# Reciprocal softmax sums applied to the outputs of two attention mixers, and a compression layer with the activations as the stationary operand

## Chip, cores and metric

The kernel runs on one core of one Trainium2 chip. The metric is the device time of one execution in microseconds; the time before is the median of three runs, 2323.13 us (2322.97 to 2323.58).

## What is computed

One sequence of 512 positions and 1024 features, in fp32, goes through two layers of a first block (compressed, selected and windowed attention, a linear recurrence and a convolution) and then through a second block of two layers, each with a mixer, a cross attention and a feed-forward part. The change touches two pieces of this. The compression, in each layer of the first block, for keys and for values:

```
def compress(kv, pos, w1, w2):
    blk = (kv[:, :, idx] + pos).reshape(B, N_KV, n_cmp, L_CMP * HEAD_DIM)
    return jax.nn.silu(blk @ w1) @ w2
...
kc = compress(k_c, cmp_pos[0], cmp_w1[0], cmp_w2[0])
vc = compress(v_c, cmp_pos[1], cmp_w1[1], cmp_w2[1])
```

There are 31 windows of 32 positions for each of two heads, so `blk @ w1` has an inner size of 2048 and 256 outputs. And the attention of the two mixers (two branches of 8 heads each):

```
s = jnp.einsum('bqhgd,bkhd->bhgqk', q_blk, k, preferred_element_type=jnp.float32) * scale
p = jax.nn.softmax(s, axis=-1).astype(v.dtype)
return jnp.einsum('bhgqk,bkhd->bqhgd', p, v)
```

The first mixer has a dense branch and a windowed branch with a sink; the second has a dense branch with a rotary part and a neighbourhood branch with a bias.

## The kernel before, in words

Activations lie with features on partitions and positions along the free dimension. `Net.build` (L1571) runs the stages in turn: `b0` and `b1` (two layers of the first block), `ab` (first mixer), `x0` (cross attention), `f0` (feed-forward), `cd` (second mixer), `x1`, `f1`. Python code issues instructions in program order, and a scheduling layer then puts each engine's instructions into a fixed order; on the chip each engine works through its own list and waits by semaphores.

A dense product (`dense_tile`) takes 8 blocks of 128x128 weights and for each three matmuls, high by high, high by low and low by high part (L410 to L412). `weights` (L414) loads a chunk of 8 blocks, and ScalarE and VectorE (or POOL) split it into `wh` (L432) and `wl` (L365). With `raw=True` the chunk is used in fp32 as it is; an fp32 matmul stands as two records in the trace.

`compress` (L1033) projects keys and values, adds the position terms and lays the windows out as `t2`, 128 partitions by 2 heads by 512. For each of keys and values it then does the first layer: for each half `h` of the 256 outputs and each of 16 offsets `a` one matmul with a 128x128 weight block as the stationary and 64 windows (stride 16) as the moving operand (L1063), into 64 columns of one PSUM bank. ScalarE's tanh follows. The generator yields every 8 matmuls, and strings of letters (`FIRST`, `SECOND`) say in which order the parts of the block take turns. The convolution's 31 taps run on VectorE at low priority.

`attn` (L721) handles two heads at a time, in two steps of two blocks of 128 query rows. A step issues the score matmuls (L743) into the three `s` banks, VectorE takes the row minimum of the negated scores (L754, or L750 with a mask), ScalarE the exponential with its row sum `sm` (L377), and VectorE the reciprocal `sc` (L763). The second half of a step, `attn_back` (L779), is held back by one step: it multiplies `p` by `sc` (L372, called at L793), transposes `p` in 128x128 blocks into one of two `t` banks (L798), copies that to `ptt` (L805, ScalarE), and multiplies by the values into the only `o` bank (L813), 64 partitions a head. After both steps `out_to` (L828) splits the bank into `yh` (ScalarE, L395) and `yl` (VectorE, L365), which feed the output projection.

The number `cp` in the table `CFG` says how many of 8 copies from `t` VectorE makes instead of ScalarE. `memory` (L1445) is issued after a mixer's last branch: eight casts `mh` on ScalarE (L377) and eight `ml` on VectorE (L368) for the cross attention. Then the rest of the output projection (`residual`) runs.

Of the kernel before, what the change touches and what calls it, by code (L numbers as in the profile page):

```python
# [61 lines left out]
def plan():  # L62
# [9 lines left out]
    for l in range(DEPTH):  # L72
        w = ("w_in", (l,))
        dense(f"glu{l}", *w, [c for _, _, c in _cols_in1()[:8]], kt(8))
        dense(f"ul{l}", *w, [_r(UL0 + P * c, P) for c in range(4)], kt(8))
        dense(f"kcvc{l}", *w, [_r(KC0, P), _r(VC0, P)], kt(8))
        dense(f"zl{l}", *w, [_r(ZL0 + P * c, P) for c in range(4)], kt(8))
        dense(f"zc{l}", *w, [_r(ZC0 + P * c, P) for c in range(4)], kt(8))
        dense(f"qk{l}", *w, [_r(KS0, P), _r(KW0, P)] + [_pair(Q0, j) for j in range(4)], kt(8))
        ph[f"vg{l}"] = [_blk(*w, kr, c) for kr in kt(8) for c in (_r(VS0, P), _r(VW0, P), pad24)]  # L80
        dense(f"zn{l}", *w, [_pair(ZN0, j) for j in range(4)], kt(8))
        for kv in range(2):
            ph[f"c1{l}{kv}"] = [
                _blk("cmp_w1", (l, kv),
                     np.concatenate([_r(64 * a, 64), _r(64 * (a + 16), 64)]), _r(P * h, P))
                for h in range(2) for a in range(16)]
        ph[f"c2{l}"] = (
            [_blk("cmp_w2", (l, 0), kr, np.concatenate([_r(0, 64), _r(0, 64)])) for kr in kt(2)]
            + [_blk("cmp_w2", (l, 1), kr, np.concatenate([_r(0, 64), -np.ones(64, np.int64)]))
               for kr in kt(2)])  # L90
        ph[f"lru{l}"] = [("bd", key, l, c) for c in range(4) for key in ("lru_w_a", "lru_w_i")]
        dense(f"pw2{l}", "conv_w_pw2", (l,), [_r(P * n, P) for n in range(4)], kt(4))
        nsa_rows = [_pair(0, j) for j in range(4)]
        for nm, rows in (("oc", [_r(1024 + P * k, P) for k in range(4)]),
                         ("ol", [_r(512 + P * k, P) for k in range(4)]),
                         ("ona", nsa_rows[:2]), ("onb", nsa_rows[2:])):
            dense(f"{nm}{l}", "w_out", (l,), [_r(P * n, P) for n in range(8)], rows)
# [135 lines left out]
def build_consts():  # L233
    c = Cols()
    i = np.arange(P)
    c.add("ident", np.eye(P))
    c.add("ones", np.ones((P, 1)))
# [49 lines left out]
class Net:  # L287
# [14 lines left out]
        "a": dict(lay="msssstto", spare="msss", dense="ms", tok="ssss", stat="t", ahead=1, pv=-200, sc="vvvv", cp=0, low=-4000, wp=0),  # L302
        "x": dict(lay="mmssttoo", spare="mmss", dense="ms", tok="mmss", stat="t", ahead=1, pv=-200, sc="avav", cp=0, low=-4000, wp=0),
        "f": dict(lay="mmssttoo", spare="mmss", dense="ms", tok="mmoo", stat="o", ahead=1, pv=-200, sc="avav", cp=0, low=-4000, wp=0),
        "c": dict(lay="msssstto", spare="msss", dense="ms", tok="ssss", stat="t", ahead=1, pv=-200, sc="vvvv", cp=0, low=-4000, wp=0),
# [108 lines left out]
    def weights(self, name, raw=False, keep=0):  # L414
# [5 lines left out]
        for c in range(-(-nb // cs)):  # L420
# [15 lines left out]
            for b in range(n // P):  # L436
                yield wr[:, b * P:(b + 1) * P] if raw else (wh, wl, b * P)
# [283 lines left out]
    def attn(self, heads, jr, start, stop, M, done=None, mask=None, gate=None, sink=None, order=(0, 2), pre=None):  # L721
# [7 lines left out]
        for pr in order:  # L729
# [36 lines left out]
            ends = (start and pr == order[0], stop and pr == order[1])  # L766
            step = [pre] if pre and pr == order[0] else []
# [11 lines left out]
    def attn_back(self, heads, ii, pt, sc, jr, start, stop):  # L779
        nc, pr = self.nc, ii[0]  # L780
        pts = []
        for n in range(len(heads)):
            ptt = self.pt("ptt", [P, NQ, 2 * P], F32)
            pts.append(ptt)
            for a, i in enumerate(ii):
                j0, j1 = jr(i)
                nj = j1 - j0 + 1
                p, c = pt[n, a], sc[:, n, a:a + 1]
                e = self.c["sc"][2 * n + a]
                if e == "a":  # L790
# [37 lines left out]
    def out_to(self, ys, box):  # L828
        def done():
            y = (self.r("z", "yh"), self.r("z", "yl"))  # L830
            self.split(y[0], y[1], box[0])
            ys.append(y)

        return done
# [198 lines left out]
    def compress(self, l, xhl):  # L1033
# [24 lines left out]
        for kv in range(2):  # L1058
            w = self.weights(f"c1{l}{kv}", raw=True)
            ps = self.ps("t")[:, :128]  # L1060
            for h in range(2):
                for a in range(16):
                    nc.tensor.matmul(ps[:, 64 * h:64 * h + 64], next(w), t2s[kv][:, :, a],  # L1063
                                     start=a == 0, stop=a == 15)
                    if a % 8 == 7 and h + a < 16:
                        yield
# [145 lines left out]
    def mixer_ab(self):  # L1212
# [56 lines left out]
        def band_mask(i):  # L1269
            return band[:, P if i == 0 else 0:256 if i == 3 else 384]  # L1270

        def branch(br, q, k, filler):
            ys = []
            for j in range(4):
                box, take, row = self.outs()
                hs = []
# [7 lines left out]
                if br == 0:  # L1284
                    steps = self.attn(hs, lambda i: (0, 3), True, True, 64, self.out_to(ys, box), pre=take)
                else:
                    sink = par("sink", 0, 8)[:, j::4].unsqueeze(2).to_broadcast([P, 2, 2])
                    steps = self.attn(hs, lambda i: (max(0, i - 1), min(3, i + 1)), True, True, 64, self.out_to(ys, box),
                                      pre=take, mask=lambda n, i: band_mask(i), sink=sink)
# [27 lines left out]
    def mixer_cd(self):  # L1317
# [28 lines left out]
        def d_attn(p, qkv):  # L1346
            q, k, v = qkv
            box, take, row = self.outs()
            hs, sts = [], []
# [8 lines left out]
            yield from self.attn(hs, full, True, True, 64, self.out_to(ys, box), pre=take,  # L1358
# [43 lines left out]
        def c_attn(p, fq, fk, v):  # L1402
            box, take, row = self.outs()
            hs = []
# [3 lines left out]
            yield from self.attn(hs, full, True, True, 64, self.out_to(yc, box), pre=take)  # L1408
# [224 lines left out]
```

## Time and profile before

| | |
|---|---|
| median of three runs | 2323.13 us |
| the profiled execution | 2331.09 us |
| its span, first to last instruction | 2329.3 us |
| TensorE matmul busy | 2186.1 us (94%) |
| VectorE busy | 1463.1 us (63%) |
| ScalarE busy | 961.4 us (41%) |
| POOL busy | 452.0 us (19%) |
| instructions | 29296 |

Busy time is the time in which at least one instruction of the engine runs. Matmul records overlap, since the array takes the next one before the last has left it, so the step from one start to the next says what a matmul costs. PE stands for TensorE's matmuls, PEld for its weight loads, DVE for VectorE, ACT for ScalarE, POOL for GpSimd. The letter L and a number is a line of the kernel; helpers such as `self.add` or `self.act` record their own line.

### The profile page before, as it was taken

Reading aid. Unit: us, or ns where it says so; the run is one execution under the profiler, and the core shown is the slowest. Engines: PE = TensorE matmul, PEld = TensorE weight load, DVE = VectorE, ACT = ScalarE, POOL = GpSimd, SP = SyncE. Lnnn points to the kernel's source line nnn. Section 1 sums busy time; section 2 is a strip of 40 time slices with the busy share of each in tenths; the row PEclk is TensorE's granted clock in tenths of the full one; section 3 lists DMA queues with packets and bytes.
Section 4 is the critical chain, followed back from the end, with each engine's and each line's share of the span. In section 5 each row is a group of like instructions: output and inputs, shape, how many; then the busy total and the mean of one; then the engine's idle time right before and its main releaser. Section 6 shows DMA issues by size and latency. Waiting matters only on the chain. (4 is left out here: it accounts for less than half of the span.)

```text
span 2329.3 us, 29296 instructions
## 1 busy us (share of the span) xinstructions
PE 2186.1 (94%) x11052; PEld 1739.5 (75%) x11052; DVE 1463.1 (63%) x2496; ACT 961.4 (41%) x1823; POOL 452.0 (19%) x452
## 2 busy tenths in 40 slices
PE   8898899999988999998999999999998899999998
PEld 6677766777776668666878888877766688888887
DVE  8997676598876664786565544454665555554454
ACT  4422365434234653475453222233566444322223
POOL 4533421343333133111020000011100102000002
PEclk9999899999989999999999999999999999999999
DMA  4243210233331012311323333332312132333332
GB/s 142 92 136 89 62 54 28 73 104 102 107 95 48 27 58 71 97 46 46 118 81 100 91 99 92 98 91 82 93 48 74 46 109 73 100 95 96 97 94 91
DMA packets 61436, 194.73 MB, mean 84 GB/s; under 512 B 8432, under 2 KB 10480, under 8 KB 61296
## 3 DMA queue, kind: packets, MB, share of 16 engines
q1 hardware_dynamic: 52848, 179.75, 25.7%
q10 hardware_dynamic: 8448, 13.12, 2.1%
q8 instruction: 87, 1.43, 0.3%
q14 instruction: 53, 0.43, 0.1%
HBM read 182.61 MB, written 2.10 MB: 79 GB/s over the span
## 5 line engine op out<-in xcount | busy, mean ns | idle before, releaser
L432 ACT CAST wh<-wr 128x1024 fp32r<-128x1024 f32 (+2 forms) x312 | 322.7, 1034 | 688.2 <-DMA wr<-ws 595.9
L365 DVE TENSOR_TENSOR wl<-wr,wh 128x1024 fp32r<-128x1024 f32 (+1 forms) x232 | 290.2, 1251 | 316.0 <-PE ps_m L411 143.2
L410 PE MATMUL ps_m<-xh,wh 128*128 128x512 f32 x792 | 322.8, 408 | 28.6 <-DVE z L368 12.1
L412 PE MATMUL ps_m<-xh,wl 128*128 128x512 f32 x792 | 319.2, 403 | 3.1 <-POOL wl L365 2.0
L411 PE MATMUL ps_m<-xl,wh 128*128 128x512 f32 x792 | 317.8, 401 | 2.2 <-DVE xl L368 2.2
L412 PE MATMUL ps_s<-xh,wl 128*128 128x512 f32 x696 | 274.7, 395 | 7.8 <-DVE wl L365 6.9
L365 POOL TENSOR_TENSOR wl<-wr,wh 128x1024 fp32r<-128x1024 f32 (+2 forms) x80 | 192.7, 2409 | 429.8 <-PE ps_m L411 229.5
L410 PE MATMUL ps_s<-xh,wh 128*128 128x512 f32 x696 | 274.9, 395 | 0.0
L411 PE MATMUL ps_s<-xl,wh 128*128 128x512 f32 x696 | 272.8, 392 | 0.0
L362 POOL TENSOR_TENSOR sq<-sq 128x512 f32<-128x512 f32 (+1 forms) x62 | 87.2, 1407 | 949.2 <-ACT sq L377 949.2
L410 PEld LDWEIGHTS ps_m<-xh,wh 128*128 128x128 f32 x792 | 154.2, 195 | 67.2 <-DVE z L368 13.3
L377 ACT ACTIVATE p<-ps_s,mn 128x512 f32<-128x512 f32 (+3 forms) x288 | 166.0, 580 | 58.4 <-PE ps_t L798 31.1
L412 PEld LDWEIGHTS ps_m<-xh,wl 128*128 128x128 f32 x792 | 153.7, 194 | 38.8 <-DVE wl L365 3.3
L411 PEld LDWEIGHTS ps_m<-xl,wh 128*128 128x128 f32 x792 | 153.6, 194 | 36.3 <-DVE xl L368 4.0
L368 DVE SCALAR_TENSOR_TENSOR ps_s<-up,params,ps_s 128x512 f32<-128x512 f32 x232 | 170.6, 750 | 2.7
L805 ACT COPY ptt<-ps_t 128x512 f32<-128x512 f32 (+3 forms) x288 | 131.7, 476 | 82.3 <-PE ps_t L798 80.5
L412 PEld LDWEIGHTS ps_s<-xh,wl 128*128 128x128 f32 x696 | 131.6, 189 | 38.2 <-DVE wl L365 9.4
L411 PEld LDWEIGHTS ps_s<-xl,wh 128*128 128x128 f32 x696 | 132.0, 190 | 28.2 <-issue 0.4
L410 PEld LDWEIGHTS ps_s<-xh,wh 128*128 128x128 f32 x696 | 132.1, 190 | 27.5 <-issue 0.4
L798 PE MATMUL ps_t<-consts,p 128*128 128x128 f32 x848 | 135.8, 282 | 3.7 <-ACT ptt L805 3.0
L798 PEld LDWEIGHTS ps_t<-consts,p 128*128 128x128 f32 x848 | 98.1, 141 | 44.7 <-ACT ptt L805 12.8
L362 DVE TENSOR_TENSOR X<-ps_m,X 128x512 f32<-128x512 f32 (+1 forms) x114 | 76.1, 668 | 75.1 <-PE ps_m L412 74.9
(511 smaller groups left out, 4168.9 us busy)
## 6 DMA issues: line engine op xcount, KB each, us to landing
wr<-ws SPq DMA_DIRECT2D x318, 512.0 KB, 3.6
strip<-strips ACTq DMA_DIRECT2D x8, 480.0 KB, 4.4
wr<-ws SPq DMA_DIRECT2D x8, 384.0 KB, 3.6
X<-x SPq DMA_DIRECT2D x8, 256.0 KB, 4.9
mem<-mem SPq DMA_DIRECT2D x8, 256.0 KB, 2.9
wr<-ws SPq DMA_DIRECT2D x7, 256.0 KB, 3.1
tab<-tables SPq DMA_DIRECT2D x6, 256.0 KB, 3.1
out_dram<-ox SPq DMA_DIRECT2D x8, 128.0 KB, 1.7
```

Source lines behind the costliest of these rows:

```text
L362: (eng or self.nc.vector).tensor_tensor(out=out, in0=a, in1=b, op=ALU.add)
L365: (eng or self.nc.vector).tensor_tensor(out=out, in0=a, in1=b, op=ALU.subtract)
L368: self.nc.vector.scalar_tensor_tensor(out=out, in0=a, scalar=s, in1=b, op0=op0, op1=op1)
L377: return self.nc.scalar.activation(out, in_, func, **k)
L410: mm(out, ah, bh, start=first, stop=False)
L411: mm(out, ah, bl, start=False, stop=False)
L412: return mm(out, al, bh, start=False, stop=last)
L432: nc.scalar.copy(wh[:, :n], wr[:, :n])
L798: nc.tensor.transpose(t[:, j * P:(j + 1) * P], p[:, j * P:(j + 1) * P], self.con("ident"))
L805: nc.scalar.copy(dst, src)
```

## The change

**Compression.** The weights' order in memory changes so that both column halves of an offset lie side by side. The windows of one offset (64 columns, stride 16) become the stationary operand and the 256 weight columns the moving one. Even offsets go to PSUM partitions 0 to 63, odd ones to 64 to 127. ScalarE copies the two partial sums, and two matmuls with a constant `fold` (two identities of 64 on top of each other) add them and turn them back.

**Mixers.** In the two mixers `p` is not multiplied any more. `attn` keeps the reciprocals of both steps in `inv`, and `out_to` broadcasts them with eight matmuls against the identity into a `t` bank (64 partitions a head, 128 columns a block), copies that to SBUF on ScalarE, multiplies the `o` bank by it on VectorE and splits the product. The cross attention and the first block's attention stay as they were. `cp` becomes 2 in the tables `a` (first mixer) and `c` (second mixer).

```diff
-                for h in range(2) for a in range(16)]
+                for a in range(16) for h in range(2)]
...
+    c.add("fold", (i[:, None] % 64 == np.arange(64)[None, :]).astype(np.float64))
...
-        "a": dict(lay="msssstto", spare="msss", dense="ms", tok="ssss", stat="t", ahead=1, pv=-200, sc="vvvv", cp=0, low=-4000, wp=0),
+        "a": dict(lay="msssstto", spare="msss", dense="ms", tok="ssss", stat="t", ahead=1, pv=-200, sc="vvvv", cp=2, low=-4000, wp=0),
...
-        "c": dict(lay="msssstto", spare="msss", dense="ms", tok="ssss", stat="t", ahead=1, pv=-200, sc="vvvv", cp=0, low=-4000, wp=0),
+        "c": dict(lay="msssstto", spare="msss", dense="ms", tok="ssss", stat="t", ahead=1, pv=-200, sc="vvvv", cp=2, low=-4000, wp=0),
...
-            for b in range(n // P):
-                yield wr[:, b * P:(b + 1) * P] if raw else (wh, wl, b * P)
+            for b in range(0, n // P, span):
+                yield wr[:, b * P:(b + span) * P] if raw else (wh, wl, b * P)
...
+            if inv is not None:
+                inv[pr], sc = sc, None
...
-                p, c = pt[n, a], sc[:, n, a:a + 1]
+                p, c = pt[n, a], None if sc is None else sc[:, n, a:a + 1]
...
-                if e == "a":
+                if c is None:
+                    pass
+                elif e == "a":
...
-    def out_to(self, ys, box):
+    def out_to(self, ys, box, inv=None):
+
         def done():
             y = (self.r("z", "yh"), self.r("z", "yl"))
-            self.split(y[0], y[1], box[0])
+            src = box[0]
+            if inv is not None:
+                ps = self.ps("t")
+                run = []
+                for i in range(NQ):
+                    for g in range(2):
+                        col = inv[i // 2 * 2][:, g, i % 2:i % 2 + 1]
+                        run.append(lambda i=i, g=g, col=col: self.nc.tensor.matmul(
+                            ps[64 * g:64 * g + 64, i * P:(i + 1) * P], col.to_broadcast([P, 64]),
+                            self.con("ident"), start=True, stop=True))
+                self.run_of(run)
+                rb, src = self.f("n", "ib_"), self.f("n", "yo")
+                self.nc.scalar.copy(rb, ps)
+                self.mul(src, box[0], rb)
+            self.split(y[0], y[1], src)
             ys.append(y)
...
-            w = self.weights(f"c1{l}{kv}", raw=True)
+            w = self.weights(f"c1{l}{kv}", raw=True, span=2)
+            acc = self.ps("t")[:, :256]
+            for a0 in range(0, 16, 4):
+                blocks = [next(w) for _ in range(4)]
+                run = []
+                for a in range(a0, a0 + 4):
+                    rows = slice(64 * (a % 2), 64 * (a % 2) + 64)
+                    run.append(lambda a=a, rows=rows, b=blocks[a - a0]: nc.tensor.matmul(
+                        acc[rows], t2s[kv][:, :, a], b, start=a < 2, stop=a > 13))
+                self.run_of(run)
+                if a0 < 12:
+                    yield
+            sm = self.f("d", "c1")[:, :256]
+            nc.scalar.copy(sm, acc)
             ps = self.ps("t")[:, :128]
             for h in range(2):
-                for a in range(16):
-                    nc.tensor.matmul(ps[:, 64 * h:64 * h + 64], next(w), t2s[kv][:, :, a],
-                                     start=a == 0, stop=a == 15)
-                    if a % 8 == 7 and h + a < 16:
-                        yield
+                nc.tensor.matmul(ps[:, 64 * h:64 * h + 64], sm[:, P * h:P * h + P], self.con("fold"),
+                                 start=True, stop=True)
```

All calls of `attn` and `out_to` in `branch`, `d_attn` and `c_attn` pass `inv`.

The scheduling layer puts the instructions into these places. First, TensorE's list in the first block, where keys' compression ends (`t` is the window layout, `wr` a raw weight chunk). Before:

```order
L412 MATMUL ps_m<-xh,wl 128x512
L410 MATMUL ps_m<-xh,wh 128x512
L411 MATMUL ps_m<-xl,wh 128x512
L412 MATMUL ps_m<-xh,wl 128x512
L1063 MATMUL ps_t<-t_575,wr 128x64 x16
L410 MATMUL ps_s<-xh,wh 128x512
```

With the change:

```order
L413 MATMUL ps_m<-xh,wl 128x512
L411 MATMUL ps_m<-xh,wh 128x512
L412 MATMUL ps_m<-xl,wh 128x512
L413 MATMUL ps_m<-xh,wl 128x512
L1087 MATMUL ps_t<-wr,t_575 64x256 x8
L411 MATMUL ps_s<-xh,wh 128x512
```

The place is the same; 16 matmuls with 64 columns became 8 with 256 columns on half of the partitions. Over the whole list there are 14 such groups, of 4 or 8.

Second, ScalarE's list at the end of the first mixer: `ptt` are the copies of transposed rows, `mh` the casts of the memory, `ib_` the copy of the broadcast reciprocals. Before:

```order
L805 COPY ptt<-ps_t 128x3x128
L377 ACTIVATE mh<-mem,params 128x256 x3
L805 COPY ptt<-ps_t 128x2x128
L377 ACTIVATE mh<-mem,params 128x256 x5
L395 CAST yh<-ps_o 128x512
L1477 COPY RBm<-ps_t 128x256
```

With the change:

```order
L811 COPY ptt<-ps_t 128x2x128
L811 COPY ptt<-ps_t 128x3x128
L378 ACTIVATE mh<-mem,params 128x256 x8
L850 COPY ib__9441<-ps_t 128x512
L396 CAST yh<-yo 128x512
L378 ACTIVATE msq<-mem 128x512 x2
```

All eight casts now stand between the last copy of transposed rows and the copy of the broadcast, and `yh` reads the product `yo`.

Third, the same list at the end of the second mixer. Before:

```order
L395 CAST yh<-ps_o 128x512
L805 COPY ptt<-ps_t 128x4x128 x5
L377 ACTIVATE mh<-mem,params 128x256 x4
L805 COPY ptt<-ps_t 128x4x128
L377 ACTIVATE mh<-mem,params 128x256 x4
L395 CAST yh<-ps_o 128x512
```

With the change:

```order
L396 CAST yh<-yo 128x512
L811 COPY ptt<-ps_t 128x4x128 x5
L378 ACTIVATE mh<-mem,params 128x256 x8
L850 COPY ib__15363<-ps_t 128x512
L396 CAST yh<-yo 128x512
```

The copy that stood between the two groups of casts is no longer there; the eight casts stand together ahead of the copy of the broadcast.

## Rows read from the trace of the kernel before

**Rows 1.** The page's first part: busy us, share of the span, instructions.
```profile
PE 2186.1 (94%) x11052; PEld 1739.5 (75%) x11052; DVE 1463.1 (63%) x2496; ACT 961.4 (41%) x1823; POOL 452.0 (19%) x452
```

**Rows 2.** Busy by stretch in the first block: PE, PEld, DVE, ACT, POOL, clock, DMA.
```profile
50.00:100.00 50.00, 44.00 (x184) 33.69 (x183) 49.52 (x65) 18.01 (x22) 29.04 (x22) 0.93 0.31 91
...
150.00:200.00 50.00, 45.32 (x213) 37.00 (x212) 46.01 (x61) 10.43 (x13) 17.50 (x10) 0.97 0.38 106
```

**Rows 3.** The same view, a stretch of the second mixer.
```profile
1750.00:1800.00 50.00, 42.91 (x225) 33.50 (x225) 30.64 (x55) 37.33 (x81) 2.59 (x5) 0.98 0.27 79
```

**Rows 4.** TensorE's waits, first mixer (961 to 1090): us, times, longest.
```profile
PE ps_s L743 <- ACT p L377: 2.5, 5, 1.0
...
PE ps_t L798 <- ACT ptt L805: 1.0, 3, 0.5
```

**Rows 5.** TensorE's waits, second mixer (1640 to 1840).
```profile
PE ps_m L410 <- ACT cf L377: 4.4, 5, 1.3
PE ps_t L1314 <- ACT cvf L1396: 4.1, 2, 2.2
PE ps_s L743 <- ACT p L377: 3.2, 5, 1.2
PE ps_o L813 <- ACT ptt L805: 2.3, 1, 2.3
```

**Rows 6.** TensorE in order of time around 16 compression matmuls: start, us, what.
```profile
126.32 0.39 PE L412 MATMUL ps_m<-xh,wl 128*128 128x512 f32 x1
126.55 3.71 PE L1063 MATMUL ps_t<-t,wr 128*128 128x64 f32 x32
...
130.35 0.39 PE L411 MATMUL ps_s<-xl,wh 128*128 128x512 f32 x1
```

**Rows 7.** The chain that ended last: start, us, what; second mixer, then cross attention.
```profile
1763.60 1.88 PE ps_o L813 x16
...
1912.95 0.86 PE ps_o L813 x4
```

**Rows 8.** TensorE in order of time around broadcasts in 64 columns (L1239).
```profile
926.09 1.97 PE L1239 MATMUL ps_t<-consts,hrs 128*64 128x128 f32 x32
...
937.72 0.39 PE L412 MATMUL ps_s<-xh,wl 128*128 128x512 f32 x1
938.03 1.09 PE L1239 MATMUL ps_t<-consts,hrs 128*64 128x128 f32 x16
...
939.39 0.40 PE L411 MATMUL ps_s<-xl,wh 128*128 128x512 f32 x1
```

**Rows 9.** Groups of instructions by form: busy us, mean ns | idle before.
```profile
L805 ACT COPY ptt<-ps_t 128x512 f32<-128x512 f32 x128 | 72.8, 590 | 27.0 <-PE ps_t L798 26.6
...
L372 DVE TENSOR_SCALAR p<-p,sc 128x512 f32<-128x512 f32 x128 | 61.6, 524 | 0.8
...
L362 DVE TENSOR_TENSOR X<-ps_s,X 128x512 f32<-128x512 f32 x62 | 42.3, 687 | 40.9 <-PE ps_s L412 40.9
```

**Rows 10.** All engines in order of time at the first mixer's end.
```profile
1078.39 0.35 ACT L805 COPY ptt<-ps_t 128x256 f32<-128x256 f32 x1
...
1078.64 2.11 ACT L377 ACTIVATE mh<-mem,params 128x256 fp32r<-128x256 f32 x5
...
1080.65 0.57 ACT L395 CAST yh<-ps_o 128x512 fp32r<-128x512 f32 x1
...
1081.27 0.78 PE L410 MATMUL ps_s<-yh,wh 128*128 128x512 f32 x1 [1.17 <-ACT yh L395]
```

**Rows 11.** The same at the second mixer's end.
```profile
1830.06 1.70 ACT L377 ACTIVATE mh<-mem,params 128x256 fp32r<-128x256 f32 x4
...
1832.28 3.60 PE L813 MATMUL ps_o<-ptt,cv 128*64 128x256 f32 x16 [2.31 <-ACT ptt L805]
...
1836.57 0.50 PE L410 MATMUL ps_s<-yh,wh 128*128 128x512 f32 x1 [0.69 <-ACT yh L395]
```

**Rows 12.** A stretch there: PE busy, granted clock, DMA share, GB/s.
```profile
1832.30:1835.60 3.30, 3.30 (x16) 0.50 0.00 0
```

More of the change, by code (lines that the diff above doesn't have):

```diff
@@ L412, in mm3, with weights @@
         return mm(out, al, bh, start=False, stop=last)
-    def weights(self, name, raw=False, keep=0):
+    def weights(self, name, raw=False, keep=0, span=1):
         cs = chunk_size(name)
@@ L718, in silu_tiles, with attn @@
             yield
-    def attn(self, heads, jr, start, stop, M, done=None, mask=None, gate=None, sink=None, order=(0, 2), pre=None):
+    def attn(self, heads, jr, start, stop, M, done=None, mask=None, gate=None, sink=None, order=(0, 2), pre=None, inv=None):
         nc = self.nc
@@ L1275, in branch @@
                 box, take, row = self.outs()
-                hs = []
+                hs, inv = [], {}
                 for g in range(2):
@@ L1284, in branch @@
                 if br == 0:
-                    steps = self.attn(hs, lambda i: (0, 3), True, True, 64, self.out_to(ys, box), pre=take)
+                    steps = self.attn(hs, lambda i: (0, 3), True, True, 64, self.out_to(ys, box, inv), pre=take, inv=inv)
                 else:
                     sink = par("sink", 0, 8)[:, j::4].unsqueeze(2).to_broadcast([P, 2, 2])
-                    steps = self.attn(hs, lambda i: (max(0, i - 1), min(3, i + 1)), True, True, 64, self.out_to(ys, box),
-                                      pre=take, mask=lambda n, i: band_mask(i), sink=sink)
+                    steps = self.attn(hs, lambda i: (max(0, i - 1), min(3, i + 1)), True, True, 64, self.out_to(ys, box, inv),
+                                      pre=take, inv=inv, mask=lambda n, i: band_mask(i), sink=sink)
                 for _ in steps:
@@ L1348, in d_attn @@
             box, take, row = self.outs()
-            hs, sts = [], []
+            hs, sts, inv = [], [], {}
             for g in range(2):
@@ L1357, in d_attn @@
                            lambda jj, rows=rows: v[:, jj, rows], row(rows), None))
-            yield from self.attn(hs, full, True, True, 64, self.out_to(ys, box), pre=take,
+            yield from self.attn(hs, full, True, True, 64, self.out_to(ys, box, inv), pre=take, inv=inv,
                                  mask=lambda n, i: sts[n][:, (7 - 2 * i) * 64:(15 - 2 * i) * 64])
@@ L1403, in c_attn @@
             box, take, row = self.outs()
-            hs = []
+            hs, inv = [], {}
             for g in range(2):
@@ L1407, in c_attn @@
                 hs.append((three(fq[g], fk[g]), lambda jj, rows=rows: v[:, jj, rows], row(rows), None))
-            yield from self.attn(hs, full, True, True, 64, self.out_to(yc, box), pre=take)
+            yield from self.attn(hs, full, True, True, 64, self.out_to(yc, box, inv), pre=take, inv=inv)
         us, cq, ckv, rot, ys, yc = ([] for _ in range(6))
```

## The prediction

> **What bounds the kernel now.** I read the page's busy shares first. TensorE is busy 94% of the span, VectorE 63%, ScalarE 41% [rows 1]: what an edit does to TensorE's own work counts nearly in full, and relief of another engine counts only where TensorE waits for that engine. So the next view is busy time by stretch. The change works in two kinds of place. In the first-part blocks, where the compression runs, VectorE is busy 49.52 and 46.01 of 50 us while TensorE is at 44.00 and 45.32 [rows 2]: there VectorE (the convolution's taps) sets the pace, and TensorE waits for it. In the second mixer VectorE falls to 30.64 of 50, ScalarE is at 37.33, TensorE at 42.91 [rows 3]: TensorE leads, and waits for ScalarE. The list of TensorE's waits there shows it: for exponentials 2.5 us in the first mixer and 3.2 in the second, for copies of transposed rows 1.0 and 2.3, for ScalarE's evacuations `cf` and `cvf` 4.4 and 4.1 [rows 4, 5], 17.5 us in all. None names the scaling of `p` on VectorE, which the change takes out.
>
> The times of this profile belong to one execution of 2331.09 us (span 2329.3 and 1.8 around it), 8.0 above the median of the runs, 2323.13. The sum below is a difference made on that execution; I put the difference onto the median. A measurement of this kernel can tell about 0.2%, 4.6 us, from no change.
>
> **Part 1, the compression's first layer.** Removed: 128 matmuls of 128 stationary columns against 64 moving ones. In the trace 16 of them (32 records: an fp32 matmul is two) stand between a dense matmul at 126.32 and the second dense one after them at 130.35 [rows 6]; two steps of dense work, 0.23 each (126.32 to 126.55), come off: 3.57 us for 16, 28.6 for 128. Added: 64 matmuls of 64 stationary columns against 256 moving ones, on alternate column halves. Their form is that of the value product, which also alternates halves: 8 of them (16 records) take 1.88 us in the chain [rows 7], so 15.0 for 64. Going into and out of that form costs a little: eight 64-column matmuls at L1239 displace 1.21 us where sixteen in a row take 0.99 for eight (worked out in part 2) [rows 8], so some 0.2 a group; the order has 14 groups, 2.8 us. The fold adds 8 matmuls of the removed size, 3.57/16 each, 1.8 us. Together 19.6 against 28.6: **9.0 us less on TensorE**. The bound on the other side is that two halves don't run side by side (the stationary operand is now read with a stride of 16, which no weight load of the trace does): two full-width matmuls with 256 moving columns, four records, took 0.86 us in the chain [rows 7], so 64 would take 27.5, and with the fold nothing is gained. I take 9.0, since the form of the value product is the same but for the stride.
>
> The Trainium skill, page "TensorEngine Tiling (Array Packing)", section Performance Considerations, recommends just this swap with two column tiles where the moving side has 64 columns or fewer, for a speedup of up to 2. By it the 28.6 would become 14.3 and not 19.6; the same page says that a change of tiling mode drains the array, and rows 8 agree, at 0.2 us a group.
>
> How much of the 9.0 reaches the end? The chunks lie where VectorE is at 92 to 99% [rows 2], and its work there is untouched: TensorE arrives earlier and waits longer. Nothing arrives if VectorE's order alone sets that stretch, all of it if TensorE does. TensorE is itself busy 88 to 91% there; I take two fifths, **-3.5 us**. The four copies of the sums and the fold sit in front of the tanh and delay it by about a microsecond; its users come later in the order and other dense tiles run meanwhile.
>
> **Part 2, the broadcasts.** Each of 16 outputs gets eight 64-column matmuls against the identity. The trace has the same form at L1239. Inside dense work eight of them displace 1.21 us (937.72 to 939.39, 1.67, less two steps of 0.23); sixteen in a row have a busy time of 1.97, 0.99 for eight [rows 8]. So 15.8 to 19.4 us; I take 1.1 each, since a part of them stands next to value products of the same tiling: **+17.6 us**. Nothing hides this: it is work of the engine that leads.
>
> **Part 3, the multiplications and copies.** 128 scalings of `p` go: 96 of 128x512 at 524 ns [rows 9], 50.3 us, and 32 narrower ones, under 0.524 each. VectorE gets 16 products from PSUM, at the 687 ns of an addition that reads PSUM [rows 9], 11.0 us, and 32 copies out of PSUM (24 full-width ones), between 524 and 687 ns each, at most 22 us. ScalarE loses the 32 copies, the 24 wide ones at 590 ns [rows 9], 14.2 us, and gains 16 of that size, 9.4. So VectorE gets some 30 us lighter, ScalarE 5 to 9. In the mixers both are cover and not the path, so this pays only through the 17.5 us of waits. With the scalings gone, VectorE starts the next minimum up to four scalings (2.1 us) earlier, and the exponentials that wait for it come earlier: I let two thirds of the 5.7 go. Of the copies' 3.3, half, since a quarter moves to a freer engine. `cf` and `cvf` queue behind weight casts and exponentials on ScalarE, which stay; of their 8.5 two fifths. Sum 8.9, **-9 us**, with ends at 0 and -17.5.
>
> **Part 4, the two mixer ends.** Here the change adds a wait. After the last value product TensorE can do little until the last `yh` is there. Before, at the first mixer's end, the last copy of transposed rows ran at 1078.39, five casts of the memory followed from 1078.64 (2.11 us, 0.42 each), then `yh` at 1080.65, and TensorE went on at 1081.27 [rows 10]: 2.5 us after that copy. Now, in ScalarE's order, eight casts stand ahead of the copy of the broadcast; 3.4 + 0.59 + 0.69 (VectorE's product) + 0.57 make 5.2, 2.7 more. At the second mixer's end the old order had four casts (from 1830.06, 1.70 us) ahead of the last copy [rows 11]; the value product came late, at 1832.28, and after TensorE's wait of 2.31 us the granted clock was 0.50 of 2.4 GHz, the 1.2 GHz level [rows 12]: its 16 records took 3.60 us, against 1.88 in rows 7, and TensorE went on at 1836.57. Now all copies stand ahead of the casts; the last, begun at 1830.06, would end at 1830.65, and the same 5.2 give 1835.9, 0.7 less. Both: **+2 us**. Behind the waiting copy stand `yh`, `yl` and the last quarter of the output projection. The 14 other outputs have transposes and dense tiles to run while the product is made: nothing.
>
> **Sum:** -3.5 + 17.6 - 9 + 2 = **+7.1 us**: 2338.2 for an execution like the profiled one, 2330.2 beside the median.
>
> **Rivals.**
> *The mixers' waits nearly all go: faster.* The end of those waits decides. With 17.5 of them gone, broadcasts at 15.8, both ends even and all 9.0 of the compression arriving, the sum is -10.7, 2312. Each stretch at 1.2 GHz that an avoided wait spares gives up to 1.7 more (3.60 against 1.88 in rows 11 and 7). It turns faster once waits and compression together give back over 24 us. For it: ScalarE queues are what TensorE waits for, and any lighter queue moves all that follows. Against it: `cf` and `cvf`, half of the sum, are not touched, and rows 2. Chance 0.28.
> *Even.* Waits and compression give back 15 to 24 us, for instance with half of the compression and 14 of the waits: 17.6 + 2 - 4.5 - 14 = +1, 2324. Another way there: the swap halves the compression, with no joints and the fold hidden, 28.6 less 15.0 [rows 6, 7], and all 13.6 arrive; with 9 of waits the sum is -3.0, 2320 (0.05 of the chance). The Trainium skill's factor of 2, in the section named above, is this case. Chance 0.28.
> *A new wait in the t banks.* The broadcast takes one of two banks that the transposes rotate through, and the only o bank is free only after VectorE's product. If each output stalls the transposes by one copy and the product, 0.59 + 0.69, the 16 cost 20 more: 2351. Against it: before, TensorE waits for copies only 3.3 us. Chance 0.06.
> *The halves don't pair.* Then the compression gives nothing: +10.6, 2334. Chance 0.06.
>
> **How the numbers follow.** Forecast case (slower, 2328 to 2338) 0.32; with the last two rivals slower is 0.44, faster 0.28, even 0.28. The forecast's own range is 2328 to 2338. The range for 8 in 10 goes from the faster rival's 2312, rounded down by one, to 2341, above the unpaired case and short of the bank case.
>
> **What would show it.** Right: the 64-column compression at about 0.235 us a matmul with pairs starting together; eight broadcasts in 1.0 to 1.2 us; longer TensorE waits for VectorE in the blocks; the mixers' stretch longer by 5 to 12 us; waits for `p` down, for `cf` and `cvf` much as before; a wait of 3 to 4 us for `yh` at the first mixer's end. Wrong: the second mixer no longer than before although 8 broadcasts stand in it, or the blocks shorter by the full 9 us.

## The result, and the profile after

The changed kernel takes 2346.0 us (median of four runs, 2343.68 to 2350.29) against 2323.36 before: ratio 1.0091, 95% interval 1.0067 to 1.0115, that is 21.1 us slower (15.6 to 26.7). The time lies above the range of 2311 to 2341. A second measurement later, on the same chip as experiments, gave 1.0061 (1.0046 to 1.0077). Slower holds in both, and the forecast of 7.1 us was too small in both.

The profiled executions are 2343.68 and 2331.09 us: the one before was high among its runs, the one after the lowest of its own. So the traces show only 12.6 us of the difference, and are read here for mechanisms, while sizes come from the comparisons. The first part of the page after, in answer to [rows 1]:

```profile
PE 2187.7 (93%) x11196; PEld 1727.5 (74%) x11196; DVE 1450.0 (62%) x2416; ACT 960.9 (41%) x1811; POOL 457.8 (20%) x452
```

TensorE's busy time grew by 1.6 us, VectorE's fell by 13, where the prediction had some 30. To see where the time went, the starts of the same weight casts (`wh`; 312 of them stand in either kernel) can be compared. From cast to cast the first block lasts 880.4 us before and 888.1 after, the first mixer 204.0 and 209.5, the second 253.5 and 257.4 (weights are cast ahead of their use, so both mixers' stretches end inside the cross attention that follows). The largest loss in these two traces is in the block, where I had expected a gain. But run 12 below is the same kernel with the same lists, and in its trace the three last 880.4, 212.3 and 259.3 us: the mixers' loss is there again, the block's is not.

TensorE's waits in the first mixer after the change (engine, tile and line that waits, what for: us in all, times, longest), in answer to [rows 4]:

```profile
PE ps_s L411 <- ACT yh L396: 2.9, 1, 2.9
...
PE ps_t L523 <- POOL rsm L360: 2.5, 1, 2.5
PE ps_s L745 <- ACT p L378: 1.5, 5, 0.4
...
PE ps_t L804 <- ACT ptt L811: 0.5, 2, 0.2
```

The same in the second mixer, in answer to [rows 5]:

```profile
PE ps_s L745 <- ACT p L378: 2.9, 3, 2.1
PE ps_m L411 <- ACT cf L378: 2.8, 4, 1.3
...
PE ps_o L819 <- ACT ptt L811: 2.0, 2, 1.4
...
PE ps_t L1345 <- ACT cvf L1427: 1.9, 1, 1.9
PE ps_m L411 <- ACT cru L378: 1.6, 1, 1.6
PE ps_t L804 <- ACT ptt L811: 1.2, 2, 1.0
PE ps_t L804 <- DVE ptt L809: 1.0, 1, 1.0
```

Exponentials and `cf` and `cvf` cost less than before, as hoped; but `cru`, copies on either engine, `yh` and `rsm` took their place.

The first mixer's end, all engines in order of time, in answer to [rows 10]:

```profile
1089.72 0.48 ACT L811 COPY ptt<-ps_t 128x384 f32<-128x384 f32 x1 [1.34 <-PE ps_t L804]
...
1090.10 3.30 ACT L378 ACTIVATE mh<-mem,params 128x256 fp32r<-128x256 f32 x8
...
1093.30 0.57 ACT L850 COPY ib__9441<-ps_t 128x512 f32<-128x512 f32 x1
1093.90 0.69 DVE L360 TENSOR_TENSOR yo<-ps_o,ib__9441 128x512 f32<-128x512 f32 x1
1094.62 0.62 ACT L396 CAST yh<-yo 128x512 fp32r<-128x512 f32 x1 [0.76 <-DVE yo L360]
...
1095.30 0.79 PE L411 MATMUL ps_s<-yh,wh 128*128 128x512 f32 x1 [2.87 <-ACT yh L396]
```

This is the queue that the prediction worked out: a copy, eight casts, the copy of the broadcast, the product, `yh`, and TensorE goes on 5.1 us after that copy's end at 1090.20 (forecast 5.2).

### The profile page after: what moved, and what is told of

The parts are those of the page before. It is cut to its first block, busy times and chain, and to the rows that moved or that the text cites. A ratio compares the mean times of both kernels' runs of the same rounds, so it can differ in the third digit from the quotient of the medians.

```text
span 2341.9 us, 29473 instructions
## 1 busy us (share of the span) xinstructions
PE 2187.7 (93%) x11196; PEld 1727.5 (74%) x11196; DVE 1450.0 (62%) x2416; ACT 960.9 (41%) x1811; POOL 457.8 (20%) x452
## 5 line engine op out<-in xcount | busy, mean ns | idle before, releaser
L811 ACT COPY ptt<-ps_t 128x512 f32<-128x512 f32 (+3 forms) x256 | 115.8, 468 | 90.9 <-PE ps_t L804 86.4
```

The lines of the kernel that those rows point to most:

```text
L811: nc.scalar.copy(dst, src)
```

## The experiments

The runs of one kernel scatter by some 15 us, so each was compared over five rounds. Microseconds are worked out as ratio times 2323; "before" is always the kernel before on the same chip.

**The two parts apart (runs 1 and 2).** Run 1 takes only the compression's hunks of the diff, run 2 only the others.

> Only the compression's part of the change; the two mixers as before. The prediction's theory (T1): TensorE saves 9 us and two fifths arrive, so 3.5 us faster than before (ratio 0.9985). Rival T2: the shorter matmuls made the scheduling layer write another order for VectorE in the first block, the product ga comes late there (TensorE waited 6.8 and 8.3 us for it in the changed kernel, 4.3 and 3.1 before), and this part is 6 to 12 us slower (ratio 1.003 to 1.005). If the mixers alone are to blame (T3), within 2 us of before.

Measured: 1.0006 (0.9988 to 1.0024), +1.4 us. The 3.5 us gain lies outside the interval.

> Only the mixers' part (reciprocals applied to the outputs, cp=2); the compression as before. T1: broadcasts +17.6, waits -9, ends +2, so 10.6 us slower (ratio 1.0046). T2, with the blocks at fault for half of the 21 us: 8 to 13 us slower as well, with the two parts adding up. T3, the mixers alone: 18 to 23 us slower (1.008 to 1.010).

Measured: 1.0069 (1.0045 to 1.0094), +16.0 us. The two add up to 17.4, between the two measurements of the whole change. T3 as stated (18 us and more, compression neutral) is near; but T1's sum for the mixers is within the interval too, so the terms had to be taken apart.

**The copies (runs 3 and 4).** Run 3 is run 2 with

```
-  "a": dict(... cp=2, ...)      "c": dict(... cp=2, ...)
+  "a": dict(... cp=0, ...)      "c": dict(... cp=0, ...)
```

> The mixers' part without the move of copies (cp=0 in both tables): ScalarE keeps all copies of transposed rows and gains the 16 copies of the broadcasts. If the copies moved to VectorE relieve TensorE's waits as the prediction has it (half of 3.3 us, plus part of cf and cvf), this is 2 to 5 us slower than the mixers' part with cp=2; if the copies on VectorE are a burden (full-width ones delay the row minima), 2 to 5 us faster than it; if neither engine is on the path, within 2 us.

Measured: 1.0056 (1.0035 to 1.0077). Against run 2 the copies are worth +3.0 us, with some 7.5 us of uncertainty: not resolved. Run 4 puts `cp=2` into the kernel before and nothing else.

> The kernel before with cp=2 alone in both mixers' tables; VectorE keeps the scalings of p and gets 32 copies on top. The prediction's view that ScalarE's queue is what TensorE waits for says 1 to 4 us faster than before; the rival, that VectorE's chain of minimum, scaling and copy is as tight, says 0 to 4 us slower.

Measured: 1.0048 (1.0029 to 1.0066), +11.2 us. Both views were wrong on size. TensorE's waits in its first mixer:

```profile
PE ps_t L798 <- DVE ptt L803: 3.2, 3, 1.9
PE ps_s L743 <- ACT p L377: 3.2, 5, 1.0
...
PE ps_t L798 <- ACT ptt L805: 1.0, 2, 0.5
```

Moved to VectorE, a copy queues behind minima and scalings (the longest of these waits ends with two copies from 984.18, behind four scalings, two minima and two other products from 980.19), and the transposes wait 3.2 us for it, a wait that did not exist; those for ScalarE's copies stay at 1.0. ScalarE got lighter (961.4 to 948.8 us in the page), and nothing came of it.

**The scalings taken out, and the broadcasts doubled (runs 5 and 6).** Run 5 is run 3 without anything in place of the scalings; run 6 is run 3 with every broadcast issued twice.

```
-            if inv is not None:
+            if False:
                 ps = self.ps("t")
```

> The mixers' part with cp=0 and without anything in place of the scalings: p is not scaled, and no broadcast, copy or product is made (left out: the division by the softmax sums in both mixers). So this is the bare gain of taking 128 scalings off VectorE. The prediction gave 9 us of waits back, some 7.4 of them without the copies: about 7 us faster than before (ratio 0.997). Rival: the scalings were hidden, and the mixers' part (13 us slower with cp=0) is the 18 us of broadcasts less little: 0 to 4 us faster than before (0.998 to 1.000).

Measured: 1.0021 (1.0002 to 1.0039), +4.9 us. There is no gain; without the 128 operations on VectorE the kernel is, if anything, a little slower. Its waits in the first mixer and then in the second:

```profile
PE ps_t L803 <- ACT ptt L810: 3.8, 2, 2.2
...
PE ps_s L744 <- ACT p L377: 1.2, 3, 0.6
```

```profile
PE ps_t L1334 <- ACT cvf L1416: 6.0, 3, 2.9
PE ps_m L410 <- ACT cf L377: 3.5, 3, 1.3
...
PE ps_m L410 <- ACT cru L377: 1.9, 1, 1.9
...
PE ps_s L744 <- ACT p L377: 1.0, 3, 0.5
```

The waits for exponentials fell as forecast, from 2.5 to 1.2 us and from 3.2 to 1.0 [rows 4, 5], 3.5 us together, and those for `cf` from 4.4 to 3.5. But others grew: the transposes wait 3.8 us for copies instead of 1.0, `cvf` takes 6.0 instead of 4.1, and `cru` is new with 1.9. Over the two mixers' stretches TensorE's named waits add up to 42.0 us before and to 41.9 here. A lighter VectorE only changed which product of ScalarE was late.

Why these were late, the trace shows too. The 3.8 us for copies are two waits, of 1.64 and 2.17 us, and the second reads:

```profile
1007.85 0.63 ACT L377 ACTIVATE msq<-mem 128x512 f32<-128x512 f32 x1 [1.69 <-DMA mem<-mem]
...
1008.39 1.06 ACT L810 COPY ptt<-ps_t 128x512 f32<-128x512 f32 x2
...
1009.01 1.27 PE L803 MATMUL ps_t<-consts,p 128*128 128x128 f32 x8 [2.17 <-ACT ptt L810]
```

The copies stand in ScalarE's list behind `msq`, a square of the memory, and ScalarE waits 1.69 us for the transfer of the memory before it can do that (1.47 us ahead of the other wait; 0.88 in all before). `cru` and `cvf` stand close behind a weight cast that waits for its transfer (1.38 us ahead of `cru`; 3.50 ahead of the longest wait for `cvf`). So what came next was not a longer row of exponentials but a transfer that ScalarE reached too early. The lists differ from those of before in other places too, and no run removed the scalings with the old order kept, so how much the new order did stays open. From cast to cast the two mixers last 454.7 us here, and 450.3 to 457.5 in the seven traces whose mixers are as before: the traces show neither gain nor loss there, and where the 4.9 us stand is open.

```
-                for i in range(NQ):
+                for i in list(range(NQ)) * 2:
```

> The mixers' part with cp=0 and each of the 16 groups of broadcast matmuls issued twice (the second writes the same values). If these matmuls lie fully on the path at 1.0 to 1.1 us a group, 16 to 18 us slower than the mixers' part with cp=0, about 29 to 31 slower than before (ratio 1.0125 to 1.0135). If part of them fills gaps in which TensorE waited anyway, 8 to 13 us more instead of 16 to 18.

Measured: 1.0083 (1.0064 to 1.0101), 6.3 us above run 3 (uncertain by 6.5; the profiled executions differ by 11.9). The second sets take 0.88 us each in the trace, 14.1 in all, so the comparison says that part of them is hidden. The traces say otherwise: from cast to cast the two mixers last 463.5 us in run 3 and 479.1 in run 6, 15.6 more. Whether a second set is hidden at all stays open. The first set of broadcasts, with its copies, products and ends, is run 3 less run 5: 8.1 us, uncertain by 6.5.

**The casts at the mixers' ends (runs 7 and 8).** The casts of the memory are ordered behind the last `yh`, in run 3 and in the kernel before.

```
+                with self.tc.issue_after(self.last["y"].ins):
                     self.split(mh[:, k % 4, :], ml[:, k % 4, :], ms[k], ...)
```

> The mixers' part with cp=0, the eight casts of the memory ordered behind the last yh of each mixer. If the mixers' ends cost what the trace of the changed kernel shows (TensorE waits 2.5 and 1.5 us for yh behind eight casts of 0.42 us), 3 to 6 us faster than the mixers' part with cp=0, so 7 to 10 us slower than before; if the casts then delay the cross attention's start or the memory's statistics (rsm, 2.5 us of wait at the first end stay), 0 to 2 us faster only.

> The kernel before with the casts of the memory ordered behind the last yh of each mixer. In its trace TensorE waits 1.17 us for yh at the first end behind five casts (2.1 us), and 2.31 us for the last copy at the second end behind four (1.7 us), with 1.7 us more at the lower clock behind that: 3 to 5 us faster than before (ratio 0.998 to 0.9987) if these lie on the path; no difference if what follows (residual tiles, the cross attention's start) waits for the casts instead.

Measured: 1.0048 (1.0030 to 1.0066) and 0.9992 (0.9980 to 1.0004), 1.9 us less in either case, neither resolved. At the first end of run 7 the wait for `yh` falls to 1.5 us, but TensorE waits 2.4 and 1.4 us for the memory's statistics (`msq` and `rsm` on POOL) right behind it: the second reading. In the changed kernel these stand behind `yh` too (the 2.5 us for `rsm` above). The order rows ahead of the prediction show it, two `msq` on ScalarE behind `yh`, and I didn't price them.

**Half of the convolution's taps (runs 9 and 10).** To see whether VectorE's amount of work eats the compression's gain, 15 of 31 taps are left out, with the old compression (run 9) and the new (run 10).

```
-                for k in range(last):
+                for k in range(1, last, 2):
```

> The kernel before with 15 of each channel group's 31 convolution taps left out (left out: half of the convolution in both layers of the first block), so that VectorE has some 90 us less to do in the first block. It is the base for the next run. If VectorE sets the pace there, TensorE's 77 us of idle time in the blocks (40.6 + 37.1 in the kernel before) fall by 15 us or more, and the time by about as much; if not, less than 5 us.

> The same with the compression's part of the change on top. If VectorE's pace took the 8 to 9 us that TensorE saved (with all taps the compression's part gave 1.4 us slower, ratio 1.0006), then here 5 to 9 us faster than the run with half of the taps and the old compression. Rival: the new form itself costs what it saves (mode changes, the copy and fold in front of the tanh, dense tiles that wait for it): within 3 us of it.

Measured: 0.9898 (0.9880 to 0.9915) and 0.9946 (0.9929 to 0.9963). Fewer taps give 23.7 us, so VectorE's list does hold TensorE up there, by its amount of work or by its order (the named waits fall by 12 us, table below). But with room on VectorE the new compression is 11.2 us slower than the old, more than its rival allowed. Run 9, the tail of the values' compression in the first layer (`h`, `v1h`, `v1l`) and the product `ga` of the convolution's last channel, which TensorE's next dense work waits for, as `ga` empties the only `m` bank:

```profile
162.88 1.93 PE L1063 MATMUL ps_t<-t,wr 128*128 128x64 f32 x16
...
164.85 0.28 ACT L377 ACTIVATE h<-ps_t 128x128 f32<-128x128 f32 x1 [0.36 <-PE ps_t L1063]
...
165.16 0.29 DVE L368 SCALAR_TENSOR_TENSOR h<-h,ps_t 128x128 f32<-128x128 f32 x1 [1.38 <-ACT h L377]
...
166.13 0.69 DVE L365 TENSOR_TENSOR v1l<-h,v1h 128x512 fp32r<-128x512 f32 x1 [0.69 <-ACT v1h L395]
...
170.34 0.69 DVE L368 SCALAR_TENSOR_TENSOR ga<-ps_m,rb 128x512 f32<-128x512 f32 x1 [1.35 <-PE ps_m L412]
...
171.17 0.47 PE L410 MATMUL ps_m<-mlh,wh 128*128 128x512 f32 x1 [0.88 <-DVE ga L368]
```

The same in run 10 (`c` is the new copy of the sums, L1076 the fold):

```profile
163.10 1.15 PE L1067 MATMUL ps_t<-wr,t 128*64 128x256 f32 x8
...
164.51 0.35 ACT L1073 COPY c<-ps_t 128x256 f32<-128x256 f32 x1
...
169.31 0.55 PE L1076 MATMUL ps_t<-consts,c 128*128 128x64 f32 x4
...
171.58 0.27 ACT L378 ACTIVATE h<-ps_t 128x128 f32<-128x128 f32 x1
...
172.85 1.78 DVE L366 TENSOR_TENSOR v1l<-h,v1h 128x512 fp32r<-128x512 f32 x1 [0.69 <-ACT v1h L396]
...
174.75 0.69 DVE L369 SCALAR_TENSOR_TENSOR ga<-ps_m,rb 128x512 f32<-128x512 f32 x1
...
175.58 0.77 PE L411 MATMUL ps_m<-mlh,wh 128*128 128x512 f32 x1 [5.20 <-DVE ga L369]
```

The window matmuls start at the same time and take 1.15 instead of 1.93 us. But behind them there are now two more steps, each in another engine's list. The copy ran at 164.51, the fold found its turn on TensorE only at 169.31, and `v1l` ended at 174.6 instead of 166.8. `ga` stands right behind `v1l` on VectorE, and TensorE waited 5.20 us for it instead of 0.88. In the changed kernel, with all taps, the same places read:

```profile
167.95 1.15 PE L1087 MATMUL ps_t<-wr,t 128*64 128x256 f32 x8
...
173.07 0.35 ACT L1093 COPY c<-ps_t 128x256 f32<-128x256 f32 x1
...
174.39 0.55 PE L1096 MATMUL ps_t<-consts,c 128*128 128x64 f32 x4
...
177.59 0.27 ACT L378 ACTIVATE h<-ps_t 128x128 f32<-128x128 f32 x1
...
180.41 0.68 DVE L366 TENSOR_TENSOR v1l<-h,v1h 128x512 fp32r<-128x512 f32 x1
...
181.21 0.69 DVE L369 SCALAR_TENSOR_TENSOR ga<-ps_m,rb 128x512 f32<-128x512 f32 x1
...
182.04 0.77 PE L411 MATMUL ps_m<-mlh,wh 128*128 128x512 f32 x1 [6.82 <-DVE ga L369]
```

Here the wait is 6.82 us, but it is 4.41 in run 12, the same kernel, and 4.38 in run 1; before it was 4.30, as `v1l` stood ahead of `ga` in the old list too. So with all taps the new tail adds little in this layer; in the second it turns 3.1 us into 5.9 (runs 1 and 12).

**The compression with the casts last, and the change once more (runs 11 and 12).** Run 11 joins the hunks of run 1 and of run 8; run 12 is the changed kernel.

> The two pieces that cost least: the compression's part of the change and the casts of the memory behind the last yh, on the kernel before. If effects add, ratio 1.0006 - 0.0008, so no change that can be told (0.9985 to 1.0015); only a ratio whose interval lies under 1 would make it a version that beats the kernel before.

> The change as it stands, on the same chip as the runs of this call. If the two parts add up (1.4 and 16.0 us), 17 us slower, ratio 1.0075; if they disturb each other, 21 us or more (1.009 and up), as the first measurement had it.

Measured: 1.0004 (0.9990 to 1.0018), no change, as the first reading had it; and 1.0061 (1.0046 to 1.0077), +14.2 us, where 17 had been expected from the sum of the parts. Nothing shows that the parts disturb each other.

**The product ahead of the tail (runs 13 to 16).** In the string of turns, the last turn of the compression (`k`) and the last of the convolution's front part (`G`) change places, and `ga` moves ahead of `h` and `v1l` on VectorE.

```
-    FIRST = "... AkOOkk/GkGONOAAQQkQAVM"
+    FIRST = "... AkOOkk/GGkONOAAQQkQAVM"
```

> The compression's part alone, with the last turn of the compression and the last turn of the convolution's front part swapped in the string of turns, so that the product ga of the last channel stands ahead of h and v1l of the values' compression in VectorE's list (places 197 and 209 where they were 201 and 200). If TensorE's saving was eaten by ga waiting behind that tail (waits of 4.4 and 5.9 us for ga in the run with the compression alone), the two waits fall to 2 us or less each and the time by 4 to 8 us: ratio 0.997 to 0.9985 against before. If VectorE's amount of work sets the end of the stretch, the waits turn up at the next product, ratio 0.999 to 1.002 as without the swap.

> The control: the kernel before with the same two turns swapped. Its waits for ga were 4.3 and 3.1 us; if the tail is what holds ga up, 2 to 5 us faster than before (0.998 to 0.999); if VectorE's amount of work is, no change that can be told.

> Half of the taps, the new compression, and the swap. Without the swap this stood at 0.9946 of before, and half of the taps with the old compression at 0.9898. If the place of ga behind the tail made the difference (waits for ga 5.2 and 4.9 us against 0.9 and 0.9), 8 to 10 us come back: ratio 0.990 to 0.9915. If the rest of the reordering did (the wait for z of 5.4 and 3.3 us at the start of the attention), less than 4 us: 0.993 to 0.995.

> The compression's part with the swap, and the casts of the memory behind the last yh: the best version the runs so far point to. If both gains hold, 2 us faster than the run with the swap alone; ratio 0.996 to 0.998 against before. If neither does, 0.999 to 1.001.

Measured against before, with TensorE's named waits of the first 890 us added up from the profiled executions:

| run | compression | taps | turns | ratio (interval) | all waits | for `ga` | for `z` |
|---|---|---|---|---|---|---|---|
| before | old | 31 | old | 1 | 82.9 | 7.4 | 18.9 |
| 1 | new | 31 | old | 1.0006 (0.9988 to 1.0024) | 92.5 | 10.3 | 18.8 |
| 14 | old | 31 | swapped | 0.9953 (0.9937 to 0.9969) | 74.3 | 0.6 | 12.3 |
| 13 | new | 31 | swapped | 0.9956 (0.9941 to 0.9970) | 76.9 | 3.0 | 9.1 |
| 9 | old | 16 | old | 0.9898 (0.9880 to 0.9915) | 70.6 | 1.7 | 11.0 |
| 10 | new | 16 | old | 0.9946 (0.9929 to 0.9963) | 81.8 | 10.1 | 18.8 |
| 15 | new | 16 | swapped | 0.9886 (0.9861 to 0.9912) | 71.5 | none | 12.6 |

With half of the taps the swap gives back 13.9 us, more than the 11.2 that run 10 lost: the order of `ga` and the tail is the likely cause there. It is not shown outright, as no run has half of the taps, the old compression and the swap; run 9 left 1.7 us of waits for `ga` to win, but 11.0 for `z`. The 13.9 are also more than the 8 to 10 expected of `ga` alone; its waits fall by 10.1 us, and those for `z` by 6.2 with them, and the two were not tried apart. With all taps, where 4 to 8 us had been expected, the swap makes the new compression 11.6 us faster than in run 1 and beats the kernel before by 10.2 us. But the control gains as much, 10.9 us where 2 to 5 had been expected: the tail held up `ga` in the old kernel too, and here as well the waits for `z` fall with it, by 6.6 us. Between runs 13 and 14 the new compression is worth nothing that can be told, as between run 1 and before. Run 16 (the swap, the new compression, the casts last) stands at 0.9960 (0.9943 to 0.9978): nothing is added by the casts. So the swap alone, run 14, beats both kernels, and needs neither part of the change.

## Why the prediction was wrong

The direction was right. Three steps failed: that two fifths of the compression's saving arrive (part 1), that nothing hides the broadcasts (part 2), and that waits taken away shorten the sum of the waits (part 3). By the terms of the sum:

| term | forecast, us | measured, us | from |
|---|---|---|---|
| compression | -3.5 | +1.4 (-2.8 to 5.6) | run 1 |
| scalings removed | -7.3 | +4.9 (0.5 to 9.1) | run 5 |
| broadcasts, ends | +17.6 + 2 | +8.1 (about 6.5 either way) | run 3 less run 5 |
| copies | -1.7 | +3.0 (about 7.5 either way) | run 2 less run 3 |
| sum | +7.1 | +17.4 | whole: 21.1 and 14.2 |

**Part 3 failed, on the mixers' waits.** The step "the exponentials that wait for it come earlier" was right on its own: three fifths of those waits went in run 5. What failed is that I let the relief end there and took the 9 us off the time: with the scalings gone TensorE's waits in the mixers add up to 41.9 us for 42.0, and the time rose by 4.9 us where 7.3 less was forecast. ScalarE came earlier to instructions that wait for a transfer, and the copies and evacuations behind them were late in place of the exponentials. I had asked of a stall that goes what is late next, for the ends and not for this term. The same holds for "a quarter moves to a freer engine": VectorE is freer on the average, not at the moment when a copy is due (run 4, in which the scalings still stand).

**Part 2 failed the other way.** TensorE spends on the broadcasts what I worked out: a group from its first start at 1040.43 to the next dense matmul at 1041.46 is 1.03 us.

```profile
1040.43 1.09 PE L845 MATMUL ps_t<-consts,sc 128*64 128x128 f32 x16
...
1041.46 0.50 PE L411 MATMUL ps_m<-yh,wh 128*128 128x512 f32 x1
```

But "nothing hides this" was wrong: even the upper bound of the measured 8.1, 14.6, lies under the 19.6 of broadcasts and ends. Where the rest went, one pair of traces shows in part. From run 5 to run 3 TensorE's waits in the two mixers' stretches fall from 41.9 to 37.3 us, and its time at 1.2 GHz from 25.0 to 14.3, which at half of the speed is some 5.4; the clock's share is not safe, as it differs by 7 us between executions of the same instructions (last section). My reading, which no run shows by itself: where TensorE soon waits anyway, a microsecond of its own work is a microsecond less of waiting. Then parts 2 and 3 rest on one mistake, made with both signs, and by luck the two errors nearly cancel: 12.3 us forecast for scalings, broadcasts and ends together, 13.0 measured. By the table, what the sum missed (10.3 us) is then the compression, 4.9, and the copies, 4.7, the latter not resolved.

**Part 1 had the price nearly right and the arrival wrong.** A group of eight old matmuls displaces 1.70 us of TensorE in the trace before (140.80 to 142.74, less a step of 0.23), one of sixteen 3.49; ten groups of the one kind, two of the other, and one each of five and eleven (1.03 and 2.38) make 27.4. With the change four matmuls displace 1.18 (152.18 to 153.59, less 0.23) and eight 2.02; twelve groups and two, 18.2; the four folds take 0.37 each, 1.5. The saving is 7.7, against my 9.0; the halves pair, and the strided stationary operand costs nothing that shows (eight in a row take 1.93 us, eight of the value product 1.88 [rows 7]). The Trainium skill's factor of up to 2 (page "TensorEngine Tiling (Array Packing)", section "Theoretical Speedup") would have made it 27.4 to 13.7; the trace shows 27.4 to 19.7 with folds. In two rows one sees the saving and that it is not kept: busy times of TensorE, its weight loads, VectorE, ScalarE and POOL in the first 890 us, before and then in run 1.

```profile
0.00:890.00 890.00, 806.43 (x4113) 629.22 (x4114) 669.10 (x1252) 376.40 (x763) 320.44 (x239) 0.95 0.27 81
```

```profile
0.00:890.00 890.00, 796.88 (x3999) 610.56 (x4000) 671.10 (x1250) 377.68 (x767) 326.45 (x238) 0.95 0.26 81
```

TensorE works 9.5 us less in the same time, and its named waits grow by 9.6. I took two fifths as arriving; in run 1 nothing did that can be told; no row stood behind the two fifths. The sentence that failed is "delay it by about a microsecond; its users come later in the order and other dense tiles run meanwhile". In run 10 the tanh starts 6.7 us later than in run 9 (171.58 and 164.85). The tail of copy, fold, tanh and `v1l` has a neighbour behind it in VectorE's list, `ga`, that TensorE needs, and I followed the tail's users but not its neighbours. Run 10 shows the price where VectorE has room, 11.2 us. With all taps, as in the changed kernel, `ga` is only a part. Of the waits that grow in run 1, 2.9 us are for `ga`, 5.9 for `mlh` and `mll`, the two parts of the recurrence's outputs, and 2.4 for the residual `X`; the rest together falls by 1.6. The first `mlh` comes 1.7 us later than before in the first layer (141.78 and 140.07) and 5.2 us later in the second (569.24 and 564.09); why, no run shows. And with `ga` ahead of the tail the saving doesn't arrive either (runs 13 and 14).

**Part 4 held for the lengths.** From the end of ScalarE's last copy to TensorE's going on it took 5.1 us at either end (1090.20 to 1095.30, 1845.05 to 1850.15) for my 5.2; I missed the `rsm` behind the first. The +2 of the sum was not measured by itself.

**The rivals.** The t banks cost little: before a broadcast TensorE waited 0.3 us for a bank in the first mixer and 0.2 in the second, and all waits for a t bank in the two, transposes and broadcasts, went from 1.7 to 3.2 us. The halves did pair. The faster case failed because the waits that went made room for others (part 3). Of the signs I named, most came: the matmuls' prices, the longer waits in the blocks, the mixers longer by 9.4 us in the traces, a wait of 2.9 us for `yh`. So they couldn't tell this outcome from the forecast. The waits for `cf` and `cvf` fell from 8.5 to 4.7 us, as the sum had it and against the sign, and yet the mixers got longer; I should have asked for the sum of the waits.

What stays open: why the two measurements of the change differ by 7 us, though their intervals overlap (in the two traces it stands in the block, where the waits for `ga` are 15.1 and 10.3 us with the same lists); whether cp=2 still costs anything once the scalings are gone; and what, besides `ga`, keeps the compression's saving from arriving with all taps.

## What to carry to other kernels

When an engine's lists are in a fixed order, price a relief by what is late next: sum all waits of the engine that leads, before and after, and not the one that you remove, and look at what the late instruction stands behind in its own list, which may be waiting for a transfer. A new step in a chain costs its place in every list that it enters; look at the instructions that stand behind the chain, not only at those that use its result. And where two stretches of work compete for one list, swapping two of them can be worth more than a cheaper form of either (here 10.9 us for two letters).

## What the hardware showed that I had not expected

**The clock.** Executions of one kernel differ by some 15 us, and part of this stands in the granted clock. The second mixer is the same instructions before and in run 1, and lasts 253.5 and 247.2 us; 17 us of it were granted at 1.2 GHz in the one and 10 us in the other, which at half of the speed is some 3.5 of the 6.3 us. The traces of before, of after and of runs 1 to 4 hold 120 to 143 us at that level; rows 12 show one such stretch, behind a wait of 2.31 us.

**VectorE beside POOL.** `v1l`, an operation on 128x512 with all operands in SBUF, took 2.71 us in the kernel before (at 176.38, while POOL ran a `wl` from 176.21 to 178.55), 1.78 in run 10 (at 172.85, beside one from 171.75 to 174.09), ending 0.54 us behind POOL's in both, and 0.69 in run 9, where POOL was idle. Over the trace before, operations that also read PSUM keep their time beside POOL: the taps have a median of 0.75 us without and with a POOL operation at the same time, the additions of 0.69; `xl`, in SBUF alone, goes from 0.74 to 1.25. The Trainium skill says so (page "SBUF — State Buffer", section "SBUF: two separate sides": an operation of VectorE with two inputs in SBUF and one of GpSimd that reads SBUF contend for a shared pair of ports, and the one that starts second waits for the whole of the other), and these rows agree.
